# First layer of a diffusion backbone: modulation, keys, values and queries in one loop over chunks of 128 features

## The chip, the core and the metric

The kernel runs on one core of a Trainium2 chip. The metric is the device time of one execution in microseconds (us). The engines are named as the profile names them: PE (TensorE, matmuls) with its weight loads PEld, DVE (VectorE), ACT (ScalarE), POOL (GpSimd), and SP, which issues the transfers.

## The reference, cut to what matters

The network has two layers over 512 tokens of 1024 features and a context of 256 tokens. The change touches the start of layer 0: a modulation (shift and scale, 1024 features each) is computed from two conditioning vectors, the normalised tokens are scaled and shifted by it, and queries, keys and values are projected.

```
m = jnp.split(silu_c @ w_ada[l] + b_ada[l], 6, axis=-1)
sh1, sc1, g1, sh2, sc2, g2 = [t[:, None, :] for t in m]
h = modulate(rms_norm(lat, g_norm1[l]), sh1, sc1)        # h * (1 + scale) + shift
csh1, csc1, ... = jnp.split(silu_cc @ w_ada[l] + b_ada[l], 6, axis=-1)
hc = modulate(rms_norm(cx, g_norm1[l]), csh1, csc1)
q, k, v, u, z = jnp.split(h @ w_in, ...)                 # q: 512 columns, k and v: 128 each, u and z: 512 each
kc, vc = jnp.split(hc @ w_in[:, Q_DIM:Q_DIM + 2 * KV_DIM], 2, axis=-1)
```

Windowed attention over q, k, v, kc, vc and a gated MLP over u and z follow, then an output projection, a mixture of 32 experts, and the second layer, which ends the same way.

## The kernel before, in words

Tokens lie in 4 blocks of 128, features in 8 chunks of 128. Every fp32 matmul that has to be exact is done as three matmuls in a faster format: `split` (L136) divides a weight into a high part (ACT copy, L139) and a low part (DVE subtraction, L140), and `mm3` (L256) multiplies high by high, high by low and low by high (L257 to L259).

The order of the work is that of the program, loosened by a scheduler that fixes one order per engine when the kernel is built. Transfers go out in order from SP. Weights land in `raw` (5 buffers of 1 MB), splits in `wp` (4 buffers). PSUM has 8 banks: `bankA` gives two banks at a time (`pa`, two buffers), `bankF` one (`pf`, two buffers), `bankP` (`pp`) and `bankO` (`po`) one each.

Layer 0 begins like this.

- `ada_rows` (L303) computes the shift, then the scale, whole: 4 tiles of 1 MB each, 8 splits, and 32 matmuls of 512 columns with only 4 weight columns (L311, L312); the row of 1024 is then turned into columns (L318) and added to the bias (L320, L321).
- Beside it the tokens arrive, `sumsq` (L221) and `rstd` (L217, on POOL) give the norm, the blocks are scaled (L334), and 32 transposes (L341) turn them into features by tokens, `xT`.
- When the whole scale is there (`gc`, L369), each chunk k is modulated: high part (ACT, L435), scaled (DVE, L436), low part (DVE, L437); keys and values of all blocks are accumulated over k in `pkv` (`kv_mm`, L403).
- Then `q_mm` (L479) does the queries block by block, 24 matmuls each, while DVE and ACT work on what is done: `kv_post` (L411) and `q_post` (L464) rotate keys and queries (`rope`, L382) and split them, `kflip` (L425) and `qflip` (L472) turn them. The context is turned, modulated and projected (`pcv`) between the queries of blocks 1 and 2.
- The attention loop (`score`, L590; its first matmul is L611, its first step on DVE the maximum L615) then runs on all engines. Between its pieces a generator, `filler` (L543), does the projections u and z from `hH` and `hL` in bank `pp`, and another, `gen0`, sums further modulation rows on DVE (L203, L205).

Of the kernel before, what the change touches and what calls it, by code (L numbers as in the profile page):

```python
# [41 lines left out]
for _n, _w in (("ident", 128), ("dup", 128), ("dup4", 128), ("io1", 128), ("io32", 32), ("io32h", 32), ("io4h", 4), ("rank", 32), ("kbrow", 32),  # L42
# [8 lines left out]
def _constants():  # L51
# [8 lines left out]
    put("ident", p == f)  # L60
    put("dup", (f % 64) == p)
# [31 lines left out]
def backbone_kernel(ctx: ExitStack, tc: tile.TileContext, a, out):  # L93
# [57 lines left out]
    first = [raw(a["wada"][0, 0, 0]), raw(a["wada"][0, 0, 1])]  # L151
    cst = cp.tile([128, NKEEP], F32)
    SP.dma_start(cst[:, 0:128], a["cst"][:, 0:128])
# [131 lines left out]
    with ExitStack() as es0:  # L285
# [15 lines left out]
        def ada_rows(s, tiles):  # L301
            pr = bankA()
            tiles = tiles + [raw(a["wada"][0, s, t]) for t in range(len(tiles), 4)]  # L303
            for t in range(4):
                w = tiles[t]
                for j in range(2):
                    k = 2 * t + j
# [30 lines left out]
        for k in range(8):  # L338
# [7 lines left out]
            if k == 3:  # L346
                take(scg, 1)
# [1216 lines left out]
```

## Time and profile before

| what | value |
|---|---|
| three timed runs | 1562.48 us median, 1560.41 to 1562.85 |
| the profiled execution | 1562.62 us, of which the span of instructions 1560.9 us |
| busy PE, DVE, ACT, POOL | 1391.3, 537.0, 356.0, 100.9 us |
| mean granted clock of PE | 0.952 |
| DMA | 508.28 MB, mean 326 GB/s |

Busy shares are means over stages with different limits. From some 320 us on most of the span is the experts' weights streaming in. The change is inside the first 107 us, so the profile is read there, stage by stage: the windows view gives busy time of each engine, granted clock (1.00 is 2.4 GHz, 0.50 is 1.2 GHz) and transfer rate of a stretch, and an x in it counts also the instructions that reach in from either end.

### The profile page before, as it was taken

What the parts mean: (1) busy time and instruction counts of PE and PEld (TensorE: products, weight loads), DVE (VectorE), ACT (ScalarE), POOL (GpSimd) and SP (SyncE); (2) the same over time, 40 slices, a digit from 0 to 9 for tenths busy, and PEclk for the clock granted to TensorE, in tenths of its full rate; (3) what the DMA queues carried; (4) which work ended last, traced back from release to release, by engine and by line L of the source; (5) the groups of instructions that cost most, each with busy time, mean ns of one, the idle gap of its engine ahead of it and who ended that gap; (6) DMA issues with size and microseconds to landing.
All of it is one profiled execution on the core that took longest, in us unless ns stands there. A gap on an engine that the chain in (4) does not pass through costs nothing. (4 is left out here: it accounts for less than half of the span.)

```text
span 1560.9 us, 18692 instructions
## 1 busy us (share of the span) xinstructions
PE 1391.3 (89%) x7260; PEld 766.0 (49%) x7261; DVE 537.0 (34%) x1103; ACT 356.0 (23%) x630; POOL 100.9 (6%) x84
## 2 busy tenths in 40 slices
PE   6899999999899999977778999989989998986775
PEld 2777667754344433421127888865444443431122
DVE  6778886642111101100028764472111111110003
ACT  6656463321010100100015333331101010100001
POOL 0000000000101011010100000000011000101100
PEclk9999899989999999999888999999999999999998
DMA  9336465598999999999994763278999999999995
GB/s 366 117 127 224 162 219 213 219 360 344 410 413 403 417 406 411 417 408 401 365 417 187 265 235 135 95 283 326 399 410 416 398 415 408 413 411 405 412 376 215
DMA packets 78672, 508.28 MB, mean 326 GB/s; under 512 B 11535, under 2 KB 11919, under 8 KB 19824
## 3 DMA queue, kind: packets, MB, share of 16 engines
q1 hardware_dynamic: 71984, 499.09, 79.3%
q0 software_dynamic: 6592, 7.92, 2.8%
q8 instruction: 59, 0.97, 0.2%
q14 instruction: 37, 0.30, 0.0%
HBM read 492.77 MB, written 19.40 MB: 328 GB/s over the span
## 5 line engine op out<-in xcount | busy, mean ns | idle before, releaser
L1219 PE MATMUL pa<-big,wp 128*32 128x512 f32 (+1 forms) x992 | 274.8, 635 | 39.8 <-DMA big<-in_wexp_dram 33.2
L1219 PE MATMUL pa<-raw,wp 128*32 128x512 f32 (+1 forms) x848 | 237.7, 645 | 28.7 <-DMA raw<-in_wexp_dram 28.7
L961 POOL DMA_INDIRECT acc<-y,ixi x60 | 89.1, 1485 | 900.3 <-DVE y L1280 684.4
L1219 PEld LDWEIGHTS pa<-big,wp 128*32 128x32 f32 (+1 forms) x992 | 69.4, 127 | 158.3 <-issue 90.5
L1146 PEld LDWEIGHTS pb<-O,big 128*128 128x128 f32 x896 | 110.8, 189 | 60.0 <-issue 55.0
L1280 DVE SCALAR_TENSOR_TENSOR y<-pa,g,g2h 128x512 f32<-128x512 f32 x26 | 19.5, 750 | 320.9 <-PE pa L1273 320.9
L1146 PE MATMUL pb<-O,big 128*128 128x256 f32 (+2 forms) x896 | 127.7, 288 | 0.0
L1219 PEld LDWEIGHTS pa<-raw,wp 128*32 128x32 f32 (+1 forms) x848 | 58.5, 128 | 128.4 <-issue 74.3
L1273 PE MATMUL pa<-big,ht 128*32 128x512 f32 (+1 forms) x496 | 107.0, 622 | 12.1 <-DMA big<-in_wexp_dram 11.9
L1234 ACT ACTIVATE gs<-pa 128x512 f32<-128x512 f32 x42 | 25.1, 597 | 378.0 <-PE pa L1219 378.0
L1273 PE MATMUL pa<-raw,ht 128*32 128x512 f32 (+1 forms) x400 | 91.0, 661 | 17.6 <-DMA raw<-in_wexp_dram 13.5
L1093 DVE TENSOR_SCALAR wp<-pb,gcol,ada 128x256 f32<-128x256 f32 (+2 forms) x64 | 31.9, 501 | 193.1 <-PE pb L1146 170.9
L140 DVE TENSOR_TENSOR wp<-raw,wp 128x1024 fp32r<-128x1024 f32 x70 | 84.0, 1220 | 36.1 <-ACT wp L139 35.4
L205 DVE SCALAR_TENSOR_TENSOR acc<-raw,csil,acc 128x1024 f32<-128x1024 f32 x70 | 89.4, 1278 | 0.6
L139 ACT ACTIVATE wp<-raw 128x1024 fp32r<-128x1024 f32 x70 | 72.0, 1053 | 43.3 <-PE pb L259 17.0
L1092 ACT ACTIVATE wp<-pb,ada,gcol 128x256 f32<-128x256 f32 (+2 forms) x64 | 33.7, 531 | 209.9 <-PE pb L1146 181.8
L1280 DVE SCALAR_TENSOR_TENSOR y<-pa,g,g2q 128x512 f32<-128x512 f32 x16 | 12.0, 750 | 180.0 <-PE pa L1273 180.0
L257 PE MATMUL pb<-big,wp 128*128 128x512 f32 x168 | 65.6, 391 | 0.0
L259 PE MATMUL pb<-big,wp 128*128 128x512 f32 x168 | 65.4, 389 | 0.0
L258 PE MATMUL pb<-big,wp 128*128 128x512 f32 x168 | 65.4, 389 | 0.0
L1241 ACT ACTIVATE sl<-pb 128x256 f32<-128x256 f32 x42 | 16.1, 382 | 203.1 <-PE pb L1237 203.1
L1273 PEld LDWEIGHTS pa<-big,ht 128*32 128x32 f32 (+1 forms) x496 | 25.5, 122 | 75.1 <-issue 41.3
(317 smaller groups left out, 1977.3 us busy)
## 6 DMA issues: line engine op xcount, KB each, us to landing
big<-in_wexp_dram SPq DMA_DIRECT2D x204, 1024.0 KB, 19.8
raw<-in_wexp_dram SPq DMA_DIRECT2D x174, 1024.0 KB, 19.8
raw<-in_wada_dram SPq DMA_DIRECT2D x48, 1024.0 KB, 5.6
raw<-in_win_dram SPq DMA_DIRECT2D x19, 1024.0 KB, 5.6
raw<-in_wout_dram SPq DMA_DIRECT2D x8, 1024.0 KB, 5.7
wp<-in_wexp_dram SPq DMA_DIRECT2D x6, 1024.0 KB, 10.4
big<-in_x_dram SPq DMA_DIRECT2D x8, 512.0 KB, 7.9
acc<-big SPq DMA_DIRECT2D x8, 512.0 KB, 2.7
```

The costliest lines, as they stand in the source:

```text
L139: A.activation(h, src, AF.Copy)
L140: V.tensor_tensor(l, src, h.bitcast(F32), OP.subtract)
L205: V.scalar_tensor_tensor(acc, src, csil[:, k, 0:1], acc, op0=OP.mult, op1=OP.add)
L257: T.matmul(po, lhsT=sH, rhs=mH, start=first, stop=False)
L258: T.matmul(po, lhsT=sH, rhs=mL, start=False, stop=False)
L259: T.matmul(po, lhsT=sL, rhs=mH, start=False, stop=last)
L961: G.indirect_dma_start(out=acc, out_offset=bass.IndirectOffsetOnAxis(ap=ix, axis=0), in_=y, in_offset=None, bounds_check=acc.shape[0] - 1, ...
L1092: return A.activation(o, src, AF.Identity, scale=g, bias=h)
L1093: return V.tensor_scalar(o, src, g, h, op0=OP.mult, op1=OP.add)
L1146: T.matmul(pg[:, :n], lhsT=src[:, b, k * 128:(k + 1) * 128], rhs=O[:, b, 0:n], start=(h == 0 and b == 0), stop=(h == 1 and b == 3))
L1219: T.matmul(pg[w * q:w * q + w, 0:512], lhsT=x[q // 2][:, k, :], rhs=ws[q][:, kk * 512:kk * 512 + 512], start=(k == 0), stop=(k == 7))
L1273: T.matmul(po, lhsT=ht[:, k, e, :], rhs=ws[e][:, c:c + 512], start=(k == 0), stop=(k == 3))
```

## The change

Shift and scale of one chunk of 128 features are computed together, in plain fp32 and without splits: `modulation(k)` takes one tile of 1 MB (`wmod`, the weights laid out by chunk), does 8 matmuls of 256 columns whose weights are 32 columns wide, four side by side in the four quarters of a bank, copies the bank on ACT, and sums the quarters and turns them with two matmuls of 2 columns against a new constant `sel`. Keys, values and queries of a chunk come from one tile (`wqk`, two chunks in 0.75 MB). `step(k)` issues the modulation of chunk k+1, the transposes of chunk k+2, the modulated chunk k, and all 12 key and value matmuls and all 12 query matmuls of chunk k; the queries of the four blocks stay in `pq` (two banks), `pp` and `po` until the last chunk. The splits of the next weights are issued behind odd chunks, the context's norm behind chunk 2, and the context's transposes and modulation, two chunks at a time, behind chunks 4 to 7. The context's projection goes to `pf`; all rotations and turns follow it. The tokens' transfers now go out ahead of the weights, and the norm is taken block by block.

```diff
-        def ada_rows(s, tiles):
...
-                    wH, wL = split(w[:, j * 1024:(j + 1) * 1024])
-                    for half in range(2):
-                        c = slice(half * 512, (half + 1) * 512)
-                        T.matmul(pr[0:4, c], lhsT=cs4[:, k, :], rhs=wH[:, c], start=(k == 0), stop=False)
-                        T.matmul(pr[0:4, c], lhsT=cs4[:, k, :], rhs=wL[:, c], start=False, stop=(k == 7))
...
+        gc = mc.tile([128, 2, 8], F32)
+        wm, wqk = {}, {}
+        def ask(k):
+            wm[k] = raw(a["wmod"][k])
+        def ask_in(j):
+            t = rawp.tile([128, 2048], F32, name="raw")
+            SP.dma_start(t[:, 0:1536], a["wqk"][j])
+            wqk[j] = t[:, 0:1536].rearrange("p (k n) -> p k n", k=2)
+        def modulation(k):
+            pr = bankF()
+            for g in range(2):
+                for q in range(4):
+                    i = 4 * g + q
+                    T.matmul(pr[32 * q:32 * q + 32, 0:256], lhsT=cs32[:, i, :], rhs=wm[k][:, i * 256:(i + 1) * 256],
+                             start=(g == 0), stop=(g == 1))
+            row = mp.tile([128, 256], F32, tag="acc", name="row")
+            A.activation(row, pr[:, 0:256], AF.Copy)
+            for s in range(2):
+                T.matmul(pr[:, 256 + 2 * s:258 + 2 * s], lhsT=row[:, s * 128:(s + 1) * 128], rhs=C("sel"), start=True, stop=True)
+            V.tensor_tensor(mod[:, :, k, :], pr[:, 256:260].rearrange("p (s n) -> p s n", s=2),
+                            bcol[:, 0, 0:2, k:k + 1].to_broadcast([128, 2, 2]), OP.add)
+            V.tensor_scalar(gc[:, :, k], mod[:, 1, k, :], 1.0, g1n[:, 0, k:k + 1], op0=OP.add, op1=OP.mult)
...
-        sh = ada_rows(0, first)
-        take(sh, 2)
+        ask(0)
+        ask_in(0)
+        ask(1)
+        ask(2)
+        ask_in(1)
...
+        def turn(k):
             p = bankF()
             for b in range(NB):
                 T.transpose(p[:, b * 128:(b + 1) * 128], x4[:, b, k * 128:(k + 1) * 128], ident)
...
+        modulation(0)
+        ask(3)
+        SP.dma_start(cst[:, 130:], a["cst"][:, 130:NKEEP])
+        SP.dma_start(rot, a["cst"][:, _C["cos"][0]:])
+        SP.dma_start(msk, a["cst"][:, NKEEP:NKEEP + 384])
+        SP.dma_start(brow, a["rows"][:, 512:592].to_broadcast([128, 80]))
         SP.dma_start(ctxb[:, :2048].rearrange("p (b d) -> p b d", b=2), a["ctx"].rearrange("(b p) d -> p b d", p=128))
-        SP.dma_start(cst[:, 128:], a["cst"][:, 128:NKEEP])
...
-        subkv = [split(wkv[:, :1024]), split(wkv[:, 1024:])]
-        gc = mc.tile([128, 2, 8], F32)
-        sc = mc.tile([128, 2, 8], F32)
-        for n in range(2):
-            V.scalar_tensor_tensor(gc[:, n], mod[:, 1, :, n], 1.0, g1n[:, 0, :], op0=OP.add, op1=OP.mult)
-            V.tensor_copy(sc[:, n], mod[:, 0, :, n])
+        turn(0)
...
+        def split_in(j):
+            w = wqk[j]
+            if j % 2 == 0:
+                t = wp.tile([128, 2048], F32R, name="wp")
+                subkv.append(t.rearrange("p (h k n) -> p h k n", h=2, k=4))
+            d = subkv[-1][:, :, 2 * (j % 2):2 * (j % 2) + 2]
+            A.activation(d[:, 0], w[:, :, 0:256], AF.Copy)
+            V.tensor_tensor(d[:, 1], w[:, :, 0:256], d[:, 0].bitcast(F32), OP.subtract)
+            t = wp.tile([128, 2048], F32R, name="wp")
+            d = t.rearrange("p (h k n) -> p h k n", h=2, k=2)
+            A.activation(d[:, 0], w[:, :, 256:768], AF.Copy)
+            V.tensor_tensor(d[:, 1], w[:, :, 256:768], d[:, 0].bitcast(F32), OP.subtract)
+            wq.append(d)
...
+        pq = bankA()
+        pqb = [pq[:, 0:512], pq[:, 512:1024], bankP(), bankO()]
+        coming = [lambda: ask(4), lambda: ask_in(2), lambda: ask(5), lambda: ask(6), lambda: ask_in(3), lambda: ask(7)]
+        split_in(0)
+        coming.pop(0)()
+        turn(1)
+        def step(k):
+            if k < 7:
+                modulation(k + 1)
+                if coming:
+                    coming.pop(0)()
+            if k < 6:
+                turn(k + 2)
+            hi = A.activation(hH[:, k, :], xT[:, k, :], AF.Identity, scale=gc[:, 0, k:k + 1], bias=mod[:, 0, k, 0:1])
+            V.tensor_scalar(xT[:, k, :], xT[:, k, :], gc[:, 0, k:k + 1], mod[:, 0, k, 0:1], op0=OP.mult, op1=OP.add)
+            lo = V.tensor_tensor(hL[:, k, :], xT[:, k, :], hH[:, k, :].bitcast(F32), OP.subtract)
             for b in range(NB):
                 kv_mm(pkv, k, b, hH, hL)
-        sub2 = splits(a["win0"][1]) + splits(a["win0"][2])
+                mm3(pqb[b], hH[:, k, tok(b)], hL[:, k, tok(b)], wq[k // 2][:, 0, k % 2], wq[k // 2][:, 1, k % 2], k == 0, k == 7)
+            with tc.issue_after(hi.ins), tc.issue_after(lo.ins):
+                if k % 2 and k < 7:
+                    split_in(k // 2 + 1)
+                    if coming:
+                        coming.pop(0)()
+                if k == 2:
+                    for b in range(2):
+                        sumsq(ss[:, 4 + b:5 + b], c4[:, b, :])
+                    rc = rstd(mc, ss[:, 4:6], 2, D)
+                    for b in range(2):
+                        V.tensor_scalar(c4[:, b, :], c4[:, b, :], rc[:, b:b + 1], None, op0=OP.mult)
+                if k >= 4:
+                    context(2 * (k - 4))
+            return hi.ins, lo.ins
+        done = step(0)
+        for k in range(1, 8):
+            with tc.issue_after(done[0]), tc.issue_after(done[1]):
+                done = step(k)
...
-        pq = bankA()
-        ks = []
-        q_mm(pq[:, 0:512], 0)
-        for n in range(NB):
-            ks.append((kv_post(pkv, n, n + 2), n + 2))
-            if n:
-                kflip(*ks.pop(0))
...
-        kflip(*ks.pop(0))
-        qs0 = q_post(pq[:, 0:512], 0)
-        q_mm(pq[:, 512:1024], 1)
-        qflip(qs0, 0)
-        qs1 = q_post(pq[:, 512:1024], 1)
-        pcv = bankA()
+        pcv = bankF()
         for k in range(8):
             for b in range(2):
                 kv_mm(pcv, k, b, hcH, hcL)
+        ks = [(kv_post(pkv, n, n + 2), n + 2) for n in range(2)]
+        qs = {0: q_post(pqb[0], 0)}
+        for k in ks:
+            kflip(*k)
         ks = [(kv_post(pcv, n, n), n) for n in range(2)]
-        pq = bankA()
-        q_mm(pq[:, 0:512], 2)
-        qflip(qs1, 1)
-        for n in range(2):
-            kflip(*ks[n])
-        qs2 = q_post(pq[:, 0:512], 2)
-        q_mm(pq[:, 512:1024], 3)
-        qflip(qs2, 2)
-        qs3 = q_post(pq[:, 512:1024], 3)
+        qflip(qs.pop(0), 0)
+        for k in ks:
+            kflip(*k)
+        for n in range(1, NB):
+            qs[n] = q_post(pqb[n], n)
+            if n > 1:
+                kflip(kv_post(pkv, n, n + 2), n + 2)
+            if n < NB - 1:
+                qflip(qs.pop(n), n)
...
+    r["wqk"] = kn(np.concatenate([we[:, 512:768], we[:, :512]], 1), 2)
+    r["win0"] = np.concatenate([kn(we[:, o:o + 512], 4) for o in (768, 1280)])
+    r["wmod"] = f("w_ada")[0, :, :2048].reshape(8, 128, 2, 8, 128).transpose(3, 1, 0, 2, 4).reshape(8, 128, 2048)
```

Two places in the fixed orders. First PE, at the first key and value matmuls (L257 before, L258 after; `raw,cs_82` are the new modulation matmuls, `cst,big` the tokens' transposes, `cst,row` the matmuls against `sel`). Before:

```order
L312 MATMUL pa<-wp,cs_86 4x512 x2
L318 MATMUL pp<-cst,row 128x4 x8
L257 MATMUL pa<-wp,big 128x256
L258 MATMUL pa<-wp,big 128x256
L259 MATMUL pa<-wp,big 128x256
L257 MATMUL pa<-wp,big 128x256
```

After the change:

```order
L320 MATMUL pf<-raw,cs_82 32x256 x8
L351 MATMUL pf<-cst,big 128x128 x3
L325 MATMUL pf<-cst,row 128x2 x2
L351 MATMUL pf<-cst,big 128x128
L258 MATMUL pa<-wp,big 128x256
L259 MATMUL pa<-wp,big 128x256
L260 MATMUL pa<-wp,big 128x256
L258 MATMUL pa<-wp,big 128x512
L259 MATMUL pa<-wp,big 128x512
L260 MATMUL pa<-wp,big 128x512
```

The queries' matmuls (512 columns) now stand among the keys' and values' (256 columns), and the next chunk's modulation and transposes stand ahead of each chunk.

Second DVE, at the start of attention. The first two maxima (L615 before, L645 after) stood like this, with `L140` a split for u and z and `qr`, `qs` the last block of queries:

```order
L615 TENSOR_REDUCE st<-pa 128x1
L394 TENSOR_TENSOR qr<-qr,rt 128x512
L616 TENSOR_SCALAR st<-st,brow 128x1
L140 TENSOR_TENSOR wp<-raw,wp 128x1024
L469 TENSOR_TENSOR qs<-qr,qs 128x8x64
L615 TENSOR_REDUCE st<-pa 128x1
L203 TENSOR_SCALAR acc<-raw,csil 128x1024
L616 TENSOR_SCALAR st<-st,brow 128x1
```

After the change the stretch from the first maximum on is:

```order
L645 TENSOR_REDUCE st<-pa 128x1
L388 TENSOR_TENSOR kr<-kr,rt 128x128
L646 TENSOR_SCALAR st<-st,brow 128x1
L141 TENSOR_TENSOR wp<-raw,wp 128x1024
L525 TENSOR_TENSOR qs<-qr,qs 128x8x64
L414 TENSOR_TENSOR ks<-kr,ks 128x2x128
L382 TENSOR_TENSOR qr<-po,rot 128x512
L386 TENSOR_TENSOR rt<-po,rot 128x16x16 x2
L382 TENSOR_TENSOR kr<-pa,rot 128x128
L388 TENSOR_TENSOR qr<-qr,rt 128x512
L386 TENSOR_TENSOR rt<-pa,rot 128x4x16 x2
L141 TENSOR_TENSOR wp<-raw,wp 128x1024
```

Five more rows follow (two splits of L141, and L525, L388, L414) before the second L645; from there the two orders read alike for the next rows (L203, L616, L205 before; L204, L646, L206 after). Thirteen rows stand between the last context value's projection and the first L645 (rotations of the third key block and of the second and third query blocks, and the context's keys).

## Rows read from the trace of the kernel before

**Rows 1.** The windows view, two stretches: span, then busy us (x instructions) of PE, PEld, DVE, ACT, POOL, granted clock, DMA share, GB/s.

```profile
0.00:42.80 42.80, 26.52 (x113) 10.22 (x114) 27.33 (x40) 28.66 (x38) 1.22 (x6) 0.92 0.95 369
101.20:245.00 143.80, 134.00 (x807) 98.64 (x805) 119.50 (x212) 86.76 (x163) 1.01 (x1) 0.96 0.62 220
```

**Rows 2.** The groups of instructions by form, 0 to 102 us: splits of weights.

```profile
L140 DVE TENSOR_TENSOR wp<-raw,wp 128x1024 fp32r<-128x1024 f32 x25 | 29.6, 1219 | 9.0 <-ACT wp L139 8.5
L139 ACT ACTIVATE wp<-raw 128x1024 fp32r<-128x1024 f32 x26 | 26.2, 1050 | 10.3 <-DMA raw<-in_wada_dram 5.8 <-PE pa L259 4.3
```

**Rows 3.** The timeline: start us, us, engine, line, what, [idle before].

```profile
7.03 2.00 ACT L139 ACTIVATE wp<-raw 128x1024 fp32r<-128x1024 f32 x2 [3.98 <-DMA raw<-in_wada_dram]
...
42.80 0.39 PE L257 MATMUL pa<-wp,big 128*128 128x256 f32 x1 [1.52 <-ACT big L435]
...
101.24 0.36 PE L611 MATMUL pa<-raw,big 128*128 128x256 f32 x1
...
105.84 0.68 DVE L615 TENSOR_REDUCE st<-pa 128x1 f32<-128x512 f32 x1
```

**Rows 4.** The windows view: the transfer rate of 8 to 16 us, and PE from 30 to 40 us.

```profile
8.00:16.00 8.00, 6.10 (x16) 1.47 (x16) 4.86 (x5) 7.34 (x12) 0.00 (x0) 1.00 1.03 417
30.00:40.00 10.00, 8.31 (x37) 2.30 (x35) 9.58 (x13) 7.65 (x10) 0.00 (x0) 1.00 0.98 368
```

**Rows 5.** The groups of instructions by form, 0 to 102 us: operations ahead of the keys and values.

```profile
L221 ACT ACTIVATE junk<-big 128x1024 bf16<-128x1024 f32 x6 | 6.3, 1051 | 0.1
L435 ACT ACTIVATE big<-big,sc,gc 128x512 fp32r<-128x512 f32 x8 | 5.8, 801 | 0.4 <-DVE gc L369 0.4
L437 DVE TENSOR_TENSOR big<-big 128x512 fp32r<-128x512 f32 x8 | 5.1, 686 | 0.0
L436 DVE TENSOR_SCALAR big<-big,gc,sc 128x512 f32<-128x512 f32 x8 | 4.0, 542 | 0.0
L334 DVE TENSOR_SCALAR big<-big,rs 128x1024 f32<-128x1024 f32 x4 | 2.7, 749 | 1.1 <-POOL rs L217 1.1
L345 DVE COPY big<-pf 128x512 f32<-128x512 f32 x4 | 2.7, 684 | 1.3 <-PE pf L341 1.3
L217 POOL TENSOR_TENSOR rs<-ms,mh 128x4 f32<-128x4 f32 x1 | 1.0, 1012 | 16.0 <-DVE ms L215 16.0
```

**Rows 6.** The windows view: PE's pace on keys and values, then on queries.

```profile
42.80:50.60 7.80, 6.42 (x29) 6.21 (x30) 7.80 (x16) 7.77 (x12) 0.00 (x0) 0.57 0.65 255
50.76:58.66 7.90, 7.90 (x68) 7.90 (x67) 4.99 (x10) 1.04 (x2) 0.70 (x1) 1.00 0.39 135
78.76:80.90 2.14, 2.14 (x7) 1.65 (x6) 0.38 (x2) 0.00 (x0) 0.00 (x0) 0.50 0.77 222
84.11:88.20 4.09, 4.09 (x20) 3.33 (x18) 0.07 (x1) 0.00 (x0) 0.00 (x0) 1.00 0.01 4
```

**Rows 7.** The timeline of PE: transposes and narrow matmuls.

```profile
92.72 1.03 PE L476 MATMUL pf<-cst,qs 128*128 128x128 f32 x8
...
396.83 4.46 PE L1219 MATMUL pa<-big,wp 128*64 128x512 f32 x18
401.21 3.07 PE L1273 MATMUL pa<-raw,ht 128*32 128x512 f32 x20
```

**Rows 8.** The page's costliest groups: busy us, mean ns of one.

```profile
L1273 PE MATMUL pa<-raw,ht 128*32 128x512 f32 (+1 forms) x400 | 91.0, 661 | 17.6 <-DMA raw<-in_wexp_dram 13.5
```

**Rows 9.** The groups of instructions by form, 0 to 102 us: DVE's work on keys and queries.

```profile
L388 DVE TENSOR_TENSOR qr<-pa,rot 128x512 f32<-128x512 f32 x4 | 2.8, 689 | 7.0 <-PE pa L259 7.0
L422 DVE TENSOR_TENSOR ks<-kr,ks 128x256 fp32r<-128x256 f32 x6 | 2.5, 422 | 0.3 <-ACT ks L421 0.2
L392 DVE TENSOR_TENSOR rt<-pa,rot 128x256 f32<-128x256 f32 x6 | 2.2, 414 | 0.0
L392 DVE TENSOR_TENSOR rt<-pa,rot 128x64 f32<-128x64 f32 x8 | 1.6, 215 | 0.0
L388 DVE TENSOR_TENSOR kr<-pa,rot 128x128 f32<-128x128 f32 x4 | 1.2, 291 | 2.7 <-ACT vS L413 2.5
```

More of the change, by code (lines that the diff above doesn't have):

```diff
@@ L150, in backbone_kernel @@
     SP.dma_start(par, a["par"])
-    first = [raw(a["wada"][0, 0, 0]), raw(a["wada"][0, 0, 1])]
     cst = cp.tile([128, NKEEP], F32)
-    SP.dma_start(cst[:, 0:128], a["cst"][:, 0:128])
+    SP.dma_start(cst[:, 0:130], a["cst"][:, 0:130])
     xb = big()
@@ L327, in backbone_kernel @@
         xT = v8(xTt)
-        sh = ada_rows(0, first)
-        take(sh, 2)
+        ask(0)
[3 more added lines that the diff above has]
+        ask_in(1)
+        gsg = mc.tile([128, 512], F32, name="gsg")
+        rot = mc.tile([128, 512], F32, name="rot")
+        msk = mp.tile([128, 384], F32, tag="P", name="msk", bufs=5)
+        ctxb = big()
         for b in range(NB):
             sumsq(ss[:, b:b + 1], x4[:, b, :])
-        r0 = rstd(mc, ss[:, 0:4], 4, D)
-        for b in range(NB):
-            V.tensor_scalar(x4[:, b, :], x4[:, b, :], r0[:, b:b + 1], None, op0=OP.mult)
-        take(sh, 3)
-        scg = ada_rows(1, [])
-        take(scg, 1)
-        for k in range(8):
+            r0 = rstd(mp, ss[:, b:b + 1], 1, D)
+            V.tensor_scalar(x4[:, b, :], x4[:, b, :], r0, None, op0=OP.mult)
+        def turn(k):
             p = bankF()
@@ L431, in kflip @@
                 A.activation(kT[g][:, :, tok(s)], pt[:, g * 256:g * 256 + 256].rearrange("p (h n) -> p h n", h=2), AF.Copy)
-        pkv = bankA()
-        for k in range(8):
-            A.activation(hH[:, k, :], xT[:, k, :], AF.Identity, scale=gc[:, 0, k:k + 1], bias=sc[:, 0, k:k + 1])
-            V.tensor_scalar(xT[:, k, :], xT[:, k, :], gc[:, 0, k:k + 1], sc[:, 0, k:k + 1], op0=OP.mult, op1=OP.add)
-            V.tensor_tensor(hL[:, k, :], xT[:, k, :], hH[:, k, :].bitcast(F32), OP.subtract)
+        subkv = []
@@ new lines, in context @@
+        def context(k):
+            p = bankF()
+            for j in range(2):
+                for b in range(2):
+                    T.transpose(p[:, j * 256 + b * 128:j * 256 + b * 128 + 128], c4[:, b, (k + j) * 128:(k + j + 1) * 128], ident)
+            A.activation(cT2[:, k:k + 2, :], p.rearrange("p (j n) -> p j n", j=2), AF.Copy)
+            for k in (k, k + 1):
+                A.activation(hcH[:, k, :], cT2[:, k, :], AF.Identity, scale=gc[:, 1, k:k + 1], bias=mod[:, 0, k, 1:2])
+                V.tensor_scalar(cT2[:, k, :], cT2[:, k, :], gc[:, 1, k:k + 1], mod[:, 0, k, 1:2], op0=OP.mult, op1=OP.add)
+                V.tensor_tensor(hcL[:, k, :], cT2[:, k, :], hcH[:, k, :].bitcast(F32), OP.subtract)
@@ L441, in backbone_kernel @@
+            return hi.ins, lo.ins
[3 more added lines that the diff above has]
+                done = step(k)
+        held = []
+        for _ in range(2):
+            t = rawp.tile([128, 2048], F32R, name="raw")
+            held.append(t)
+        kT = [t[:, 0:1536].rearrange("p (h n) -> p h n", h=2) for t in held]
+        SP.dma_start(gsg, a["rows"][:, 0:512].to_broadcast([128, 512]))
         wsp = mc.tile([128, 8, 128], F32)
@@ L533, in filler @@
         def filler():
-            for part, dst in ((5, z), (3, u)):
+            for part, dst in ((2, z), (0, u)):
                 sub = splits(a["win0"][part]) + splits(a["win0"][part + 1])
@@ L546, in filler @@
                     yield
-                if part == 3:
+                if part == 0:
                     A.activation(uz[:, :2048], uz[:, :2048], AF.Gelu)
```

84 lines of the change are left out of this document (15 added, 69 removed).

## The prediction

> **What bounds the kernel now.** I read the windows view first. Up to 42.8 us the transfers are busy for 0.95 of the time, but DVE is busy for only 27.3 us and PE for 26.5 [rows 1]: the stage is a chain. The whole shift and scale must arrive, be split, multiplied and turned before the first chunk can be modulated. The groups show the price of the splits: 1.22 us on DVE and 1.05 on ACT for each 1024 columns, 16 of them for shift and scale [rows 2]. The timeline gives the two marks that I use: the first key matmul starts at 42.80, and waited for ACT's modulated chunk 0; the first score starts at 101.24, and the second block's maximum on DVE at 105.84 [rows 3]. From there to 245 us PE is busy for 134.0 of 143.8 us and DVE for 119.5 [rows 1], so neither has much room. Everything later follows from the end of that stage, by buffers that come free; I let it move along unchanged. The sum is made against the profiled execution, 1562.62 us, which is 0.14 above the median of the runs (1562.48).
>
> **The start, up to the first key matmul.** In the profiled execution the first 1.14 MB (two small loads and one weight tile) had landed at 7.03 [rows 3]. Now the tokens are first: with the constants 2.25 MB, so 1.11 MB more, at 417 GB/s [rows 4] 2.7 us: the last block lands at 9.7, the first modulation tile (1.05 MB) at 12.2. The last block's square sum takes 1.05 and its read-out 0.2, POOL's power about 1.0 with 0.3 of handing over, the scaling 0.75 [rows 5]: 13.0. The modulation of chunk 0 has 8 matmuls of 256 columns. The nearest row is 20 narrow ones of 512 columns in 3.07 us, 0.154 each, so 0.077 for half the columns [rows 7]; at the lower clock level, with which PE begins, 0.154, and 1.2 us for the eight: 13.6 with the way out. The copy, the two small matmuls and the bias bring that to 14.5. DVE then has a split's low halves (1.8 for 1536 columns, by rows 2), the small columns 0.3, the copy of the turned chunk 0.68: 17.4. ACT's high part takes 0.80, then DVE scales in 0.54 and subtracts in 0.69 [rows 5]: 19.4. So the first chunk begins at 19.4 instead of 42.8.
>
> **The eight chunks on PE.** Keys and values: 66 starts in 7.90 us, 0.120 each; queries: 18 starts in 4.09 us, 0.227 each [rows 6] (the x of the rows counts also what reaches in from the ends). 96 of each: 11.5 + 21.8 = 33.3 us, as before. New between them, for six chunks: the modulation 0.6, four transposes 0.5 (8 take 1.03, rows 7), the two small matmuls 0.3 (priced as transposes), and some 0.3 of waiting for ACT's copy, since the transposes cover only a part of it: 1.7, so 10 us. The context's 16 transposes add 2.1. After the idle start PE ran for 7.8 us at a mean of 0.57 [rows 6]; I count the same once, 4 us. The last chunk ends at 19.4 + 33.3 + 10 + 2.1 + 4 = 68.8.
>
> The price of a modulation is the uncertain one. From below it is 0.6 us as taken. From above, if the four quarters did not run side by side, eight times half of the 0.661 us that one narrow matmul lasts [rows 8]: 2.6, so 2 more for each chunk, 14 in all. I take the lower end, since the rows of narrow matmuls are the same shape in the same quarters. A change between full and narrow matmuls costs nothing in the trace: the narrower kind starts at 401.21, before the last of the wider kind ends (396.83 + 4.46 = 401.29) [rows 7]. TensorEngine Tiling in the Trainium skill (Tiling Modes, Key Properties) says that changing the tiling mode drains the engine. By that rule 16 changes at 0.661 - 0.154 = 0.5 us would add 8 us, and the time would be 1557.5; the trace does not agree with it, and no sum here uses it.
>
> **The context and the rotations.** 48 matmuls at 0.120 are 5.7 us: 74.5. In the kernel before the rotations lay beside the queries' matmuls; now they all come behind the last chunk, and so do the four splits for u and z. This is the term that gives back. DVE still has, after the context's projection and before the second maximum (the order shows the rows): three blocks of queries at 0.69 + 2 x 0.41 + 0.69 + 0.69 = 2.9, so 8.7; two blocks of keys at 0.29 + 2 x 0.215 + 0.29 + 0.42 = 1.4, so 2.9; the context's keys 1.4; one maximum with its bound 0.9 [rows 9, 3]; four splits 4.9 [rows 2]. That is 18.8, a little less as records overlap (25 x 1.219 is more than the 29.6 that rows 2 show): 18. The second maximum starts at 74.5 + 0.2 + 18 = 92.7, against 105.84. PE cannot run ahead meanwhile: its order is fixed, the second score needs the two banks that hold the keys until the third and fourth key blocks are rotated, u and z need bank `pp` and the splits, and the mix needs `po`. From the second maximum on the orders are alike, so the shift of 13.1 us goes through: 1562.62 - 13.1 = 1549.5.
>
> **Edits at nothing.** Transfers: up to the last modulation tile 16.4 MB must land, at 417 GB/s some 39 us after a start at about 4: 43, wanted at about 56. Their issue on SP stands behind waits for `raw` buffers, which modulations and splits free a chunk or more earlier; if that cover went, each late tile would stop one chunk. The norm by block costs POOL three more calls, under 1.0 us each [rows 5], beside later blocks' arrival. The 16 splits that vanish are on ACT and DVE in a stage where now PE sets the pace (per chunk DVE has about 4 us of work, PE 6).
>
> **The rivals.**
> *The backlog is absorbed.* If DVE makes good its late rotations in the 24 us that it idles from 101.2 to 245 [rows 1], what counts is PE at the first score. That needs the context's keys, about 5 us after 74.5, so 79.7 against 101.24; PE then still has 24 transposes more to do (3.1 us, rows 7): a gain of 18.4, 1544.2. For it: the idle time; against: PE waits for exactly that work, in a fixed order.
> *The chunks are bound by the chain.* ACT's copy of a modulation stands behind a split's high halves (1.6 us by rows 2) in three chunks, and the start is late by 3 more: 8 us, 1557.5.
> *PE stays at the lower clock.* Each chunk has pauses around its modulation. If they hold the clock at 0.50, queries take 0.428 instead of 0.227 (5 starts in 2.14 us, rows 6), 19.3 us more, and keys, small matmuls, and the context's projection double: 11.5 + 12 + 5.7, less the 4 counted: 44.5 us, 1594. It decides from 26 us of lower clock beyond the 7.8 counted, since each costs half of itself. Against it: from 30 to 40 us PE was busy 8.31 of 10 us in short pieces, with the clock at 1.00 [rows 4]. TensorE: Matmul & The Clock Gate in the Trainium skill (A second HAM failure mode) tells of a kernel whose cycling through PSUM banks left small pauses in which the clock swung back. By that rule this rival would be the forecast; rows 4 show pauses without it.
> *The change does not do what it says.* If a buffer or an order holds the chunks back until all tiles are in, the time stays near 1562.
>
> **How the numbers follow.** Forecast 0.60, backlog absorbed 0.18, chain 0.12, lower clock 0.07, no effect 0.03. The range takes in the first three with their bounds, from 1540 (absorbed, and a start some 4 us earlier in all) to 1557.5 (chain); the doubled price of the modulation lies just outside. About 0.2%, 3.1 us, is what a measurement of this kernel can tell from no change. Faster by more: 0.88; within: 0.04; slower: 0.08.
>
> **What would show it.** Right: the first chunk's key matmul near 19 us, eight chunks of some 6 us each, the last ending near 69 at clock 1.00, the first score near 80, the second maximum near 93, DVE without a pause between the last two. Wrong: the narrow fp32 matmuls of one chunk taking over 2 us, the clock at 0.50 past the second chunk, PE waiting inside chunks for ACT or DVE, or later stages that do not begin 13 us earlier.

## The result, and the profile after

The changed kernel took 1550.44 us (median of five, 1545.57 to 1553.35), the kernel before beside it 1562.48 (1560.41 to 1562.85): a ratio of 0.9924, 95% interval 0.9903 to 0.9945. The forecast was 1549.5. The profiled execution of the changed kernel is its shortest, 1545.57, with a span of 1543.3 us. One execution of twelve of the variant e4_mod_first below took 2224.35 us at a granted clock of 0.56; its ratio leaves it out.

The windows view of the changed kernel, over its own marks (span, then busy us of PE, PEld, DVE, ACT, POOL, granted clock, DMA share, GB/s): up to the first key matmul, the chunks, up to the first score, up to the second maximum, and from the first score to the end of the mix:

```profile
0.00:21.76 21.76, 8.29 (x52) 5.02 (x54) 7.88 (x20) 9.75 (x17) 2.41 (x9) 1.00 0.89 352
21.76:71.34 49.58, 49.58 (x348) 39.03 (x348) 25.25 (x59) 21.41 (x36) 0.70 (x1) 1.00 0.65 247
71.34:82.79 11.45, 9.51 (x77) 8.50 (x75) 9.87 (x29) 7.64 (x22) 0.00 (x0) 1.00 0.01 1
82.79:95.13 12.34, 9.52 (x55) 7.24 (x56) 12.00 (x26) 11.03 (x21) 0.00 (x0) 1.00 0.20 64
82.79:237.00 154.21, 140.58 (x846) 103.07 (x847) 127.63 (x230) 96.08 (x181) 1.01 (x1) 0.97 0.57 205
```

The long chain at the start [rows 1] is gone: through all eight chunks PE has no pause (49.58 of 49.58 us), while DVE and ACT are busy for about half of it (25.25 and 21.41 us). Then the bound changes hands: up to the second maximum DVE is busy for 12.00 of 12.34 us and PE waits.

The timeline of PE, with the second maximum on DVE:

```profile
12.79 1.93 PE L320 MATMUL pf<-raw,cs 128*32 128x256 f32 x16 [12.79 <-DMA raw<-in_wmod_dram]
...
18.34 1.93 PE L320 MATMUL pf<-raw,cs 128*32 128x256 f32 x16 [0.69 <-ACT big L353]
20.21 0.90 PE L351 MATMUL pf<-cst,big 128*128 128x128 f32 x3
20.90 0.89 PE L325 MATMUL pf<-cst,row 128*128 128x2 f32 x4
21.66 0.45 PE L351 MATMUL pf<-cst,big 128*128 128x128 f32 x1
21.76 0.56 PE L258 MATMUL pa<-wp,big 128*128 128x256 f32 x1
...
22.55 0.63 PE L258 MATMUL pa<-wp,big 128*128 128x512 f32 x1
22.97 0.63 PE L259 MATMUL pa<-wp,big 128*128 128x512 f32 x1
...
25.85 0.40 PE L258 MATMUL pp<-wp,big 128*128 128x512 f32 x1
26.09 0.40 PE L259 MATMUL pp<-wp,big 128*128 128x512 f32 x1
...
27.68 1.07 PE L320 MATMUL pf<-raw,cs 128*32 128x256 f32 x16
28.69 0.66 PE L351 MATMUL pf<-cst,big 128*128 128x128 f32 x4
29.26 0.61 PE L325 MATMUL pf<-cst,row 128*128 128x2 f32 x4
29.73 0.36 PE L258 MATMUL pa<-wp,big 128*128 128x256 f32 x1
...
34.10 1.07 PE L320 MATMUL pf<-raw,cs 128*32 128x256 f32 x16
...
95.13 0.68 DVE L645 TENSOR_REDUCE st<-pa 128x1 f32<-128x512 f32 x1
```

Read it by differences of starts. A chunk is 34.10 - 27.68 = 6.42 us: modulation 1.01, transposes 0.57, small matmuls 0.47, keys, values and queries 4.37. The first modulation and the first half of chunk 0 run at half that pace: 1.93 against 1.07, and 512 columns in 0.42 (22.55 to 22.97) against 0.24 (25.85 to 26.09). The first key matmul starts at 21.76 where it was 42.80, and the second maximum at 95.13 where it was 105.84 [rows 3], 10.7 us earlier. The last mix of layer 0 moves from 247.82 to 237.17, so the shift is carried through. The profiled end moves by 17.1; what of that is this change, the first experiment asks.

### The profile page after: what moved, and what is told of

It reads as the page before. It is cut to its first block, busy times and chain, and to the rows that moved or that the text cites. A ratio compares the mean times of both kernels' runs of the same rounds, so it can differ in the third digit from the quotient of the medians.

```text
span 1543.3 us, 18848 instructions
## 1 busy us (share of the span) xinstructions
PE 1383.5 (90%) x7340; PEld 766.7 (50%) x7341; DVE 520.0 (34%) x1097; ACT 342.6 (22%) x621; POOL 102.7 (7%) x87
## 5 line engine op out<-in xcount | busy, mean ns | idle before, releaser
L1249 PE MATMUL pa<-raw,wp 128*32 128x512 f32 (+1 forms) x848 | 241.1, 647 | 24.6 <-DMA raw<-in_wexp_dram 21.2
L1303 PE MATMUL pa<-raw,ht 128*32 128x512 f32 (+1 forms) x400 | 85.1, 613 | 18.8 <-DMA raw<-in_wexp_dram 14.8
L206 DVE SCALAR_TENSOR_TENSOR acc<-raw,csil,acc 128x1024 f32<-128x1024 f32 x70 | 89.4, 1278 | 1.1 <-DMA raw<-in_wada_dram 0.5
L141 DVE TENSOR_TENSOR wp<-raw,wp 128x1024 fp32r<-128x1024 f32 x48 | 58.1, 1220 | 26.7 <-ACT wp L140 26.6
L258 PE MATMUL pb<-big,wp 128*128 128x512 f32 x168 | 65.7, 391 | 0.0
L140 ACT ACTIVATE wp<-raw 128x1024 fp32r<-128x1024 f32 x48 | 49.8, 1057 | 33.0 <-PE pb L260 17.0
## 6 DMA issues: line engine op xcount, KB each, us to landing
big<-in_wexp_dram SPq DMA_DIRECT2D x204, 1024.0 KB, 19.4
```

Source lines behind the costliest of these rows:

```text
L140: A.activation(h, src, AF.Copy)
L141: V.tensor_tensor(l, src, h.bitcast(F32), OP.subtract)
L206: V.scalar_tensor_tensor(acc, src, csil[:, k, 0:1], acc, op0=OP.mult, op1=OP.add)
L258: T.matmul(po, lhsT=sH, rhs=mH, start=first, stop=False)
L1249: T.matmul(pg[w * q:w * q + w, 0:512], lhsT=x[q // 2][:, k, :], rhs=ws[q][:, kk * 512:kk * 512 + 512], start=(k == 0), stop=(k == 7))
L1303: T.matmul(po, lhsT=ht[:, k, e, :], rhs=ws[e][:, c:c + 512], start=(k == 0), stop=(k == 3))
```

## The experiments

All kernels are edits of the changed kernel. The marks come from one profiled execution each (us from the span's start): end of the last chunk, second and fifth maximum, last mix of layer 0, first narrow expert matmul on a raw tile; then that execution's time and the median of the runs.

| kernel | last chunk | max 2 | max 5 | last mix | expert | profiled | median |
|---|---|---|---|---|---|---|---|
| before | - | 105.84 | 113.63 | 247.82 | 385.21 | 1562.62 | 1562.48 |
| changed | 71.34 | 95.13 | 102.67 | 237.17 | 374.02 | 1545.57 | 1550.44 |
| e0_again | 71.43 | 96.42 | 103.95 | 239.93 | 377.30 | 1551.52 | 1551.43 |
| e1_split_early | 71.42 | 93.76 | 101.67 | 237.62 | 374.34 | 1547.96 | 1546.97 |
| e1_once_more | 72.09 | 95.57 | 103.48 | 238.94 | 375.52 | 1549.97 | 1548.37 |
| e2_mod_twice | 80.21 | 104.02 | 111.56 | 247.64 | 384.63 | 1559.42 | 1555.6 |
| e3_warm | 70.43 | 94.22 | 101.77 | 239.32 | 375.99 | 1549.54 | 1549.13 |
| e4_mod_first | 81.57 | 105.36 | 113.54 | 248.95 | 385.73 | 1556.74 | 1563.58 |
| e5_low_on_pool | 71.65 | 95.52 | 104.07 | 241.18 | 378.10 | 1549.9 | 1550.64 |
| e6_early_warm | 70.66 | 93.01 | 100.91 | 236.69 | 373.41 | 1547.29 | 1547.93 |
| e7_no_turn | 70.07 | 87.72 | 99.02 | 234.90 | 371.90 | 1543.18 | 1547.85 |
| e9_ada_later | 72.63 | 94.98 | 100.24 | 236.82 | 374.78 | 1546.56 | 1544.71 |
| e12_ada_alone | 70.83 | 94.63 | 100.79 | 233.85 | 371.83 | 1543.81 | 1545.02 |
| e13_ada_two | 71.50 | 93.85 | 99.11 | 232.76 | 376.27 | 1547.89 | 1547.9 |

**The same kernel again.**

> The changed kernel once more, with nothing edited. In its profiled execution the second block's maximum came 10.7 us earlier than in the kernel before (95.13 against 105.84), the last matmul on the mix of layer 0 10.6 earlier, but the end 17.1 earlier; 6.4 of the 17.1 came in the two expert stages, where nothing is changed. Theory: the change is worth what it moves in the first stage, 10.7 us, and the rest is how far executions lie apart in the expert stages. Then the marks up to 240 us stand again within 0.5 us of those of the changed kernel, and the end lies anywhere from 1545 to 1553. Rival: the earlier start also shortens the expert stages by 6.4 us; then the shift grows from 10.7 to 17 here too, and the end is near 1545.6 again.

Measured: ratio 0.9934 (0.9921 to 0.9948). The marks up to the first maximum agree, but the second maximum is 1.3 us later, the sixteenth 4.5, the last mix 2.8. The windows view says why; of the repeat, then of the first execution:

```profile
87.00:90.00 3.00, 2.63 (x10) 2.24 (x11) 3.00 (x8) 2.38 (x5) 0.00 (x0) 0.52 0.00 0
118.00:121.00 3.00, 3.00 (x9) 2.32 (x8) 2.93 (x3) 0.93 (x4) 0.00 (x0) 0.50 0.34 52
149.00:152.40 3.40, 3.40 (x15) 1.65 (x12) 3.40 (x6) 1.97 (x5) 0.00 (x0) 0.56 0.01 2
```

```profile
87.00:90.00 3.00, 2.61 (x15) 1.96 (x16) 3.00 (x8) 3.00 (x7) 0.00 (x0) 1.00 0.00 0
116.00:120.00 4.00, 4.00 (x19) 3.29 (x18) 3.93 (x5) 1.64 (x6) 0.00 (x0) 1.00 0.30 59
```

The same program on the same data is granted the lower level (1.2 GHz) from 87 to 90, from 118 to 121 and from 149 to 152 in one execution and not in the other. In the last two PE is busy all the time; the first begins behind pauses, but the first execution has the same pauses (PE is busy for 1.30 us from 84 to 87 in the repeat, 1.29 in the first) and keeps 1.00. The first stretch is what delays the second maximum: DVE waits 1.34 us behind it for ACT, which waits for PE's slower matmuls. Neither theory foresaw this, and the rival's end near 1545.6 did not come back: marks of single executions scatter by some us from 85 us on, so small edits must be read from medians, and large ones from both. The mark of before, 105.84, is one of a single execution too, with PE at 0.50 from 78.76 to 80.90 [rows 6], so the 10.7 is good to some us. All eleven times of the changed kernel have a median of 1551.3: the change is worth 10 to 12 us, what it moved in the first stage. The profiled 17.1 was a short execution. From the first narrow expert matmul to the end, the execution of before took 1177.4 us (1562.62 - 385.21), those of the changed kernel 1171.6 and 1174.2. An earlier start need not be the reason: e4 and e2, which reach that matmul as late as before (385.73 and 384.63), took 1171.0 and 1174.8 from there. So far as single executions can tell, the one of before was long there.

**What a modulation costs.**

```
-            for g in range(2):
+            for g in (0, 1, 0, 1):
```

> Every chunk's eight modulation matmuls are issued twice over (the sum is begun anew, so the result is the same); DVE, ACT and the transfers have the same work. They took 1.0 to 1.07 us at full rate in the changed kernel's trace and about 1.9 at half. Theory (PE sets the pace of the chunks, the price of the modulation lies on the path): six chunks grow by 1.0 us each and the first two by up to 1.9, the last chunk ends 7 to 9 us later than at 71.2, and the end is later by as much, some 1558. Rival (each chunk waits for its chain through ACT's copy, DVE and back, and PE has slack): under 3 us in all, since the doubled matmuls fall into pauses.

Measured: the chunks are 38.73 - 31.45 = 7.28 us long instead of 6.42, the last ends at 80.21 (+8.9), the second maximum comes at 104.02 (+8.9), by the timeline of PE:

```profile
31.45 1.93 PE L320 MATMUL pf<-raw,cs 128*32 128x256 f32 x32
...
38.73 1.93 PE L320 MATMUL pf<-raw,cs 128*32 128x256 f32 x32
```

PE sets the pace of the chunks; the chain through ACT and DVE has slack. By the marks the theory holds up to the expert stage (384.63 against 374.02 and 377.30). The median, 1555.6 (ratio 0.9961, 0.9948 to 0.9974), is only 4.3 above the 1551.3 of the changed kernel, so part of the 8.9 was given back later or lies in the scatter; which, is not settled.

**The modulations ahead of the chunks.**

```
-            if k < 7:
-                modulation(k + 1)
...
+        for k, nxt in ((1, lambda: ask(6)), (2, lambda: ask(7)), (3, lambda: ask_in(1)), (4, lambda: ask_in(2)),
+                       (5, lambda: ask_in(3)), (6, None), (7, None)):
+            last = modulation(k)
```

> All eight modulations, still narrow and fp32, run before the first chunk; queries stay in the held banks, DVE's and ACT's work is that of the changed kernel. This undoes the pipeline over chunks alone. About 12.9 MB must land before the last modulation, 31 us at 417 GB/s after a start at 4: the first key matmul near 37 us instead of 21.8. The eight chunks lose their modulations (7 times some 1.5 us with the small matmuls and the wait) and take 39 instead of 49.4 us. Theory (the pipeline is worth what of the transfers it hides, less nothing): the last chunk ends near 76, up to 80 with stretches at half pace, the second maximum 5 to 9 us later than 95.1, the end 5 to 9 us later, some 1556 to 1560. Rival (the gain came from dropping the splits and the early tokens, and interleaving is worth nothing): within 2 us of the changed kernel.

Measured: ratio 1.0014 (1.0004 to 1.0024). Without the pipeline the whole gain is gone, more than expected (the profiled execution, 1556.74, is the shortest of the twelve). The timeline of PE, and the windows view of its chunks:

```profile
24.72 1.94 PE L320 MATMUL pf<-raw,cs 128*32 128x256 f32 x16 [0.33 <-DVE mod L326]
27.21 1.01 PE L325 MATMUL pf<-cst,row 128*128 128x2 f32 x4 [0.56 <-ACT row L323]
28.56 1.94 PE L320 MATMUL pf<-raw,cs 128*32 128x256 f32 x16 [0.33 <-DVE mod L326]
...
43.67 0.37 PE L258 MATMUL pa<-wp,big 128*128 128x256 f32 x1
```

```profile
43.67:81.57 37.90, 37.90 (x231) 33.23 (x232) 23.07 (x47) 19.37 (x31) 0.70 (x1) 1.00 0.28 99
```

The chunks did take 38 us (39 expected), but they start at 43.67 instead of 37. On its own a modulation is a little chain: 1.94 at half pace, 0.56 waiting for ACT's copy, 1.01 for the small matmuls, 0.33 for DVE, 28.56 - 24.72 = 3.84 us. In the pipeline the same costs 6.42 - 4.37 - 0.57 = 1.48, with other matmuls in the pauses and PE at full pace. Narrow fp32 matmuls in place of splits, and tokens first, bring nothing by themselves in this order, where each modulation waits for the one before: the first key matmul is back at 43.67, where it was at 42.80 [rows 3]. Modulations ahead of the chunks that overlap one another were not tried.

**PE warmed ahead of the start.**

```
+        idle = bankP()
+        for _ in range(100):
+            T.matmul(idle[:, 0:128], lhsT=onesb, rhs=onesb, start=True, stop=True)
```

> 100 small bf16 matmuls into an unused bank are put at the head of PE's program, where PE is idle until 12.79 us; nothing else is edited. In the changed kernel the first modulation took 1.93 us and the first matmuls of chunk 0 came at half pace until about 25.3; at full pace the modulation takes 1.0 and the 3.5 us of chunk 0 half as long. Theory (the half-pace start lies on the path): the first key matmul comes 0.9 us earlier, the last chunk ends 2.5 to 3 us before 71.2, and the second maximum and the end are earlier by as much, some 1548 in the median. Rival (PE idles again from 15 to 21 us, and its pace falls back): no change of the last chunk's end beyond 1 us.

Measured: ratio 0.9925 (0.9909 to 0.9941); the last chunk ends 0.9 us earlier. The rival was right, as the timeline and the windows view of this kernel show:

```profile
1.38 8.22 PE L332 MATMUL pp<-onesb 128*128 128x128 bf16 x100 [1.38 <-DVE onesb L180]
12.89 1.49 PE L320 MATMUL pf<-raw,cs 128*32 128x256 f32 x16 [3.29 <-DMA raw<-in_wmod_dram]
```

```profile
15.00:17.50 2.50, 2.30 (x10) 1.60 (x9) 1.54 (x4) 1.75 (x3) 0.00 (x0) 0.50 1.00 419
20.00:22.50 2.50, 2.50 (x12) 2.43 (x13) 1.62 (x5) 0.37 (x1) 0.00 (x0) 0.50 1.02 425
25.00:27.50 2.50, 2.50 (x26) 1.67 (x25) 1.57 (x2) 0.00 (x0) 0.00 (x0) 1.00 0.80 261
```

The small matmuls ran from 1.38 to 9.6, PE was idle for 3.29 us, and from 15 to 22.5 the granted clock was 0.50, so the rest of the start ran at half pace as before.

**DVE's row of work behind the last chunk.** Three kernels take records out of it. One leaves the rotations of blocks 1 to 3 out:

```
-            rope(qr, po, 8, b)
+            if b:
+                V.tensor_copy(qr, po)
+            else:
+                rope(qr, po, 8, b)
```

> The queries of blocks 1 to 3 are copied out of PSUM and not rotated: this leaves out part of the computation, two records of DVE per block (0.74 and 0.69 us, 1.27 from start to start), 3.8 to 4.3 us in all, all of them between the context's projection and the second maximum. Theory (DVE's backlog sets the second maximum): it comes 3.5 to 4.3 us before 95.13, near 91.2, and the end is earlier by as much, some 1546.5 in the median. Rival (PE's chain from the context's keys through the first two scores sets it, or ACT's high parts and read-outs): the second maximum moves by under 1.5 us, and DVE shows pauses of the rest between 80 and 95.

Measured: ratio 0.9915 (0.9900 to 0.9931). The second maximum came 7.4 us earlier, more than was taken out, because the order changed too and three of the four splits now stand behind it, as the timeline of DVE shows:

```profile
87.72 0.68 DVE L648 TENSOR_REDUCE st<-pa 128x1 f32<-128x512 f32 x1
...
90.90 3.49 DVE L141 TENSOR_TENSOR wp<-raw,wp 128x1024 fp32r<-128x1024 f32 x3
```

The fifth maximum, behind all of them, came 3.65 us earlier (99.02 against 102.67), the median of the time 3.5 below 1551.3. That is the theory's size.

The second splits z's first tile earlier:

```
+        wz = raw(a["win0"][2])
...
+        with tc.issue_after(done[0]), tc.issue_after(done[1]):
+            ahead = [split(wz[:, :1024]), split(wz[:, 1024:])]
...
-                sub = splits(a["win0"][part]) + splits(a["win0"][part + 1])
+                sub = (ahead if part else splits(a["win0"][part])) + splits(a["win0"][part + 1])
```

> The first weight tile for z is asked for and split right behind the last chunk, in a stretch where DVE has pauses, so that two of the four low halves (1.2 us each) leave the row of work that DVE has between the first and the second maximum. Theory (DVE's backlog sets the second maximum): the second maximum comes 1.2 to 2.4 us before 95.13, and the whole by as much, some 1549 in the median against 1550.4. Rival (PE's chain of transposes and scores sets it): the second maximum stays within 0.3 us of 95.13 and the time within 1 us of the changed kernel.

> The kernel with the early split of z's first weight tile, unchanged, timed again, since its first four times (median 1546.97) stood 3.5 to 4.5 us below the changed kernel's while its second maximum was only 1.4 to 2.7 us earlier. If the edit is worth what the second maximum moved, its median is 1548 to 1550 here; if it is worth the whole, 1547 again, and the mark of the last matmul of layer 0's mix is 3.5 us or more ahead of the changed kernel's where the lower clock took equally long in both.

Measured: 1546.97 (ratio 0.9903, 0.9888 to 0.9918), then 1548.37 (0.9914, 0.9898 to 0.9929). The second maximum moved to 93.76 in the first execution. In the second it stood at 95.57, with the granted clock at 0.66 from 80 to 85. Over all nine times the median is 1547.8, 3.5 below the changed kernel, more than the 1.4 us that the mark moved; the sign is sure, the size is not.

The third gives the low parts to POOL (both subtractions as G.tensor_tensor):

> The subtractions that make the low parts of the rotated keys and queries go from DVE to POOL, which is idle there (0.00 us busy from 58 to 95). On DVE they were 0.69 us for each of four query blocks and 0.42 for each of six key blocks, 5.3 us, 3.9 of it in records between the first score's work and the second maximum or just ahead. Theory (DVE's backlog): the second maximum comes 3 to 4 us before 95.1 if a subtraction on POOL takes no more than twice as long as on DVE. Rival (the subtraction is on the chain from the context's projection to the first score, where POOL is slower): the first score comes 1 to 3 us after 82.8, and the second maximum gains nothing.

Measured: ratio 0.9941 (0.9924 to 0.9958), no gain. The timeline of POOL, then of DVE, then the windows view:

```profile
74.39 0.74 POOL L414 TENSOR_TENSOR ks<-kr,ks 128x256 fp32r<-128x256 f32 x1 [0.55 <-ACT ks L413]
...
89.13 0.72 POOL L414 TENSOR_TENSOR ks<-kr,ks 128x256 fp32r<-128x256 f32 x1
```

```profile
74.51 0.90 DVE L452 TENSOR_TENSOR big<-big 128x256 fp32r<-128x256 f32 x1
...
75.99 0.41 DVE L452 TENSOR_TENSOR big<-big 128x256 fp32r<-128x256 f32 x1
...
83.66 0.68 DVE L388 TENSOR_TENSOR qr<-qr,rt 128x512 f32<-128x512 f32 x1
...
89.39 1.01 DVE L388 TENSOR_TENSOR qr<-qr,rt 128x512 f32<-128x512 f32 x1
...
95.52 0.69 DVE L645 TENSOR_REDUCE st<-pa 128x1 f32<-128x512 f32 x1 [1.32 <-PE pa L644]
```

```profile
90.00:93.00 3.00, 3.00 (x12) 2.60 (x13) 2.03 (x6) 2.09 (x4) 0.00 (x0) 0.50 0.71 300
```

The subtraction takes 0.74 us on POOL instead of DVE's 0.42 [rows 9], and while it runs the same record of DVE is longer: 0.90 against 0.41, 1.01 against 0.68. The first score was late by only 0.2 us (82.97), so the rival's place was wrong too. The second maximum waited 1.32 us for PE's score, which it had not before. Two things stand ahead of that wait. The way through POOL is longer: PE starts to turn the second block's queries at 85.52, where the changed kernel does at 84.40. And in this execution PE was granted 0.54 from 87 to 94.5, where the changed kernel had 1.00. One profile does not say what each took, so why the median gained nothing stays open. SBUF — State Buffer in the Trainium skill (two separate sides) says that a DVE operation with two SBUF inputs and a GpSimd operation that reads SBUF exclude each other on a shared pair of ports; both records shown are of that kind, so the trace agrees. A DVE record that reads PSUM kept its length beside POOL: 0.67 at 87.93, with POOL at work from 87.89.

Both additions of the early split and the small matmuls in one kernel:

> The early split of z's first weight tile and the matmuls at the head of PE's program in one kernel. Theory (the two act on different stretches, the start and the row of DVE's work behind the last chunk): their gains add, the second maximum near 91, and the end 4 us before the changed kernel, some 1547. Rival (with an earlier last chunk the tile for z has not been split in DVE's pauses, or lands late): no better than the better of the two.

Measured: 1547.93 (ratio 0.9919, 0.9904 to 0.9934), no better than the early split alone (1547.8 over nine), as the rival says. The second maximum stood at 93.01, where the theory said 91: 0.75 us before the first execution of the early split alone, as the last chunk is (70.66 for 71.42).

**The row continues behind the second maximum.** Between the second and the fifth maximum of the changed kernel DVE also multiplies adaLN weights for later, by its timeline:

```profile
96.52 1.28 DVE L206 SCALAR_TENSOR_TENSOR acc<-raw,csil,acc 128x1024 f32<-128x1024 f32 x1
97.71 0.69 DVE L645 TENSOR_REDUCE st<-pa 128x1 f32<-128x512 f32 x1
...
100.13 1.28 DVE L206 SCALAR_TENSOR_TENSOR acc<-raw,csil,acc 128x1024 f32<-128x1024 f32 x1
...
101.44 1.28 DVE L206 SCALAR_TENSOR_TENSOR acc<-raw,csil,acc 128x1024 f32<-128x1024 f32 x1
102.67 0.69 DVE L645 TENSOR_REDUCE st<-pa 128x1 f32<-128x512 f32 x1
```

Keeping them out of the first unit of scores is one line (n counts the units):

```
-                if i % 2 or i == 0 and n % 2:
+                if n and (i % 2 or i == 0 and n % 2):
                     take(gen0, 1)
```

With the early split:

> The kernel with the early split of z's first weight tile, and besides the adaLN products that DVE does for later layers (records of 1.27 us) are not interleaved with the first four scores any more, but begin with the second unit. Theory (DVE still sets the pace for some 10 us behind the second maximum): three to four of the 1.27 us records leave the row between the second and the fifth maximum, which comes 1.5 to 4 us before the 101.7 of the kernel with the early split alone, and since DVE has pauses later that take them up, 1 to 3 us stay to the end, some 1545 in the median. Rival (from the second maximum on PE with the matmuls for u and z sets the pace, or the moved products push later splits and maxima by as much): the sixteenth maximum stays within 0.5 us of 152.0 less what stretches at half clock differ, and the end within 1 us of 1547.

Alone, and with the second unit left out too (n > 1):

> The changed kernel with the adaLN products of later layers kept out of the first unit of scores, without the early split. With both edits the median was 1544.7, with the early split alone 1547.0 and 1548.4, with neither 1550.4 and 1551.4. Theory (both edits take records of DVE out of its full row behind the last chunk, and add): some 1548 here, and the fifth maximum 1.5 to 3 us before 102.7. Rival (the products can only give way because the early split made room): within 1 us of the changed kernel, 1550 to 1551.5.

> As the kernel with the early split and the products kept out of the first unit, but out of the second as well. Theory (behind the first unit DVE has pauses anyway, so there is nothing more to win): within 1 us of 1544.7, and later if the products are then late for the end of the stage, where the last mix would come behind 236.8. Rival (DVE still sets the pace in the second unit): 1.5 to 2.5 us earlier, 1542.5 to 1543.5.

Measured: 1544.71 (ratio 0.9887, 0.9870 to 0.9905) with the split, 1545.02 (0.9893, 0.9876 to 0.9909) alone, 1547.9 (0.9903, 0.9887 to 0.9920) with two units. The one line beats both kernels, by 5 to 6 us against the changed one; its theory said 3, and the early split adds nothing measurable to it. Its last mix comes at 233.85, 3.3 us earlier; its last maximum comes 2.4 us earlier (220.64 for 223.04), with about as much lower clock ahead of it (8.0 us for 7.5, in windows of 0.5 us). So the marks bear out the theory's 3, and the rest of the median's gain is not explained. With two units the mix ends earlier still (232.76), but the time is some 3 us longer, which the theory had only for a last mix behind 236.8. The last of the products on DVE, and the windows view behind the last mix, in the one-unit kernel and then in the two-unit kernel:

```profile
244.67 1.28 DVE L206 SCALAR_TENSOR_TENSOR acc<-raw,csil,acc 128x1024 f32<-128x1024 f32 x1
234.00:244.50 10.50, 10.50 (x61) 9.12 (x60) 9.44 (x15) 0.73 (x1) 0.00 (x0) 1.00 0.67 234
```

```profile
255.97 1.28 DVE L206 SCALAR_TENSOR_TENSOR acc<-raw,csil,acc 128x1024 f32<-128x1024 f32 x1
233.00:243.50 10.50, 10.50 (x41) 9.44 (x41) 7.22 (x12) 2.53 (x3) 0.00 (x0) 0.52 0.57 212
243.50:297.00 53.50, 53.50 (x295) 45.81 (x295) 35.56 (x85) 18.76 (x37) 1.94 (x4) 1.00 0.59 217
```

The last product ends 11.3 us later, and the experts start 4.4 us later, 5.5 more behind the last mix (143.5 for 138.0). But the trace does not show the late products as the cause: PE is busy without a pause from 233 to 297, and it runs at 0.52 up to 243.5, where the one-unit kernel has 1.00, which is worth about 5 us (10.5 x 0.48). Whether the other executions of the two-unit kernel lost their 3 us in the same way, these runs do not show.

## Why the prediction was right, step by step

*The start* was 2.4 us late, 21.76 for 19.4. The first tile came at 12.79 instead of 12.2, and its modulation took 1.93 instead of 1.2. The chain through ACT's high part and DVE's low part, by their timelines:

```profile
19.02 0.81 ACT L470 ACTIVATE big<-big,mod,gc 128x512 fp32r<-128x512 f32 x1 [0.73 <-DVE big L355]
20.45 0.69 DVE L472 TENSOR_TENSOR big<-big 128x512 fp32r<-128x512 f32 x1
```

It was done at 21.14, 1.7 us after the sum's 19.4. The rest is a term that the sum left out: in PE's order the second modulation, transposes and small matmuls stand ahead of the key matmuls (18.34 to 21.76), at half pace.

*The chunks* took 49.6 us against 49.4, by errors that cancel. The eight narrow matmuls cost 1.01 us, not 0.6: the price from the expert stage's rows [rows 7], halved for half the columns, was too low, though nearer than the upper end of 2.6. That is 2.4 us in six chunks; the small matmuls (0.47 for 0.3) add 1.0, and keys, values and queries, 4.37 a chunk for 4.16 (33.3 / 8), 1.7. Against it, half pace cost 27.68 - 21.76 - 4.37 = 1.55 instead of 4, and the wait of 0.3 for ACT's copy never came, as PE had no pause; the context's transposes took 0.5 less, as the last four fall behind the chunks. The doubled modulation shows that this price lies on the path.

*The context and the backlog* were right. From the end of the context's projection (77.52) to the second maximum 17.6 us passed, for 18.2 in the sum, DVE busy nearly throughout; leaving 4 us of it out made 3.5. PE and ACT follow closely: in the repeat the second maximum waited for them. So the second maximum is late by what the last chunk is late (71.34 for 68.8), and the shift is 10.7, not 13.1. That it goes through unchanged holds up to the expert stage.

*The rivals.* "Bound by the chain" fell for the chunks, where PE has no pause; its late start (3 us) came near, with 2.4. "Lower clock" fell where I put it: behind the first half of chunk 0 the chunks run at full pace, by the column and by the starts. The small pauses between groups of which the Trainium skill tells (TensorE: Matmul & The Clock Gate, A second HAM failure mode) do not occur in the chunks. The lower stretches came later, one behind pauses that did no harm in the other execution and two with PE busy, so these traces do not settle whether pauses bring them. The drain between tilings of which the Trainium skill tells (TensorEngine Tiling, Tiling Modes, Key Properties) is not in the rows either: the narrow matmuls' record ends at 28.75, the next transposes start at 28.69. The prediction took rows 7 for a change between full and narrow matmuls, but both of their records are narrow, with 64 and 32 weight columns (`128*64`, `128*32`); the change to full width is seen only here. "The backlog is absorbed" did not happen. Moving the adaLN products gave 1545.0, close to that rival's 1544.2, but not by its way: the second maximum stayed at 94.63. The time itself, 0.9 us from the forecast, is closer than the steps deserve, by luck: errors of 1 to 2.5 us cancelled.

## What to carry to other kernels

Putting a serial preparation into the loop it prepares pays here because it fills pauses and keeps PE at full pace; the cheaper form of the preparation by itself, in one row ahead of the loop, gained nothing. When the results of a loop are held until its end, everything that used to lie beside it becomes one row on another engine: list that row from the order, and first move out of it what nobody needs yet. Before small edits are judged, the unchanged kernel should be profiled twice, and before a lost or won microsecond is put down to an edit, the granted clock of that stretch should be compared in both kernels.

## What was not expected of the hardware

- One kernel is granted the lower clock in different places from execution to execution, also where PE is busy throughout: 118 to 121 at 0.50 in one, 1.00 there in the other. The marks come 1.3 to 1.6 us later behind each of the three stretches of 3 to 4 us, nearly half their length.
- The granted clock's column reads 1.00 over the first 21.76 us of the changed kernel, yet the same record lasts 1.93 us at 12.79 and 1.07 at 27.68. In that stretch the distance between starts is the evidence, not the column.
- POOL and DVE are not independent: beside a POOL subtraction of 0.74 us a DVE record with two inputs in SBUF lasted 0.90 instead of 0.41.
